# A state space scan on one core: its decay matrices made by small TensorE products in PSUM

## The chip, the core and the metric

The kernel runs on one core of a Trainium2 chip. The metric is the time of one execution in device microseconds. Before the change three runs took 1881.87 to 1888.46 us, with a median of 1887.11 us.

## What is computed

One layer of a hybrid block over 1024 tokens of width 1024, with 256 context tokens in front of the state space branch: a norm, three parallel branches (a bidirectional Mamba-2 scan, a Fourier mixing and a spatial gating), their gated merge, and a gated MLP. The change touches the scan alone. Its core, for one direction:

```python
def ssd_scan(x, dt, a, bm, cm, init_state, with_y):
    xf = (x.astype(jnp.float32) * dt[..., None]).reshape(b, nc, Q, G, R, P)
    la = jnp.transpose((dt * a).reshape(b, nc, Q, G, R), (0, 3, 4, 1, 2))
    cum = jnp.cumsum(la, axis=-1)
    ...
    tri_q = jnp.tril(jnp.ones((Q, Q), dtype=bool))
    lmat = jnp.exp(jnp.where(tri_q, cum[..., :, None] - cum[..., None, :], -jnp.inf))
    cb = jnp.einsum('bcqgn,bcsgn->bcgqs', cf, bf)
    y_diag = jnp.einsum('bcgqs,bgrcqs,bcsgrp->bcqgrp', cb, lmat, xf)
    y_off = jnp.einsum('bcqgn,bcgrpn,bgrcq->bcqgrp', cf, prev, jnp.exp(cum))
    y = (y_diag + y_off).reshape(b, L, H, P)
    return y.astype(x.dtype), final

def ssd_bidir(xs, bm, cm, dt, a_log, init_f, init_b, with_y):
    a = -jnp.exp(a_log.astype(jnp.float32))
    flip = lambda t: jnp.flip(t, axis=1)
    y_f, s_f = ssd_scan(xs, dt[:, :, 0], a[0], bm, cm, init_f, with_y)
    y_b, s_b = ssd_scan(flip(xs), flip(dt[:, :, 1]), a[1], flip(bm), flip(cm), init_b, with_y)
```

There are 16 heads in two groups of eight, and eight chunks of 128 tokens. lmat is the decay matrix: one 128 x 128 matrix for each head, chunk and direction.

## The kernel before

Activations lie with channels on the 128 partitions and tokens along the row. A big product is one output tile of 128 channels by 1024 tokens: eight slices of the inner dimension, each as three fp32r products (high by high, high by low, low by high) of two halves of 512 columns, 48 products in all (`mm3`, lines 147 to 157). It accumulates in a tile of two PSUM banks, `ps_big`, from a pool of two such tiles. psx, psf, psz, psu and psv are such accumulators: convolution inputs of the scan (psx), the Fourier branch (psf), the scan's gate (psz) and the two halves of the spatial gating (psu, psv). The weights come through `win`, which loads a tile, rounds it on ScalarE and takes the low part on GpSimd.

The scan runs in `ssd_group`, once per group of heads. Per chunk c it forms pcb (B by C of the chunk, L550), cbm (pcb under both triangular masks, L552), the contribution of the running state (`y_off`: po on TensorE, times the exponentiated rows ro, L514 to L519), and for each half group hg of four heads the weights E: rows of cumulated decays, broadcast over all partitions, come from memory by `rload` (rf and rs, L495); each head gets ScalarE L561, VectorE L562 (the smaller of both directions' exponents), ScalarE L564 and VectorE L565 (G: the masked cb times the step sizes of both directions). One Exp (L567), one multiplication on GpSimd (L568), and four heads of products into py (L573). Then y is added (L576), and the states of both directions go one chunk further (`state_step`, pS on TensorE L527, GpSimd L524 and L529, VectorE L531); the backward direction works on chunk 7 - c in the same turn. The row vectors ro have two buffers, the loads of x for the backward direction (Xb) one.

The order on each engine is not that of the text: a scheduler rearranges the instructions of the whole program by a model of their times, within what buffers and data allow, and each engine then works through its list in order. Buffers of a pool go to the tiles in the order in which the text allocates them. In the text `ssd_group(0)` comes first, then `group_in(1)` (psx9, psf0, psx11, psf1, psx4, psf2, psx5, psf3, psx6, psx7), then `ssd_group(1)`, then psz0 to psz3, psu0 to psu3 and psv0 on. Ahead of `ssd_group(0)` stand the last context tile (psc7) and `ctx_state`, which makes four start states through one tile and stores each (Std).

## Time and profile before

| | |
|---|---|
| median of three runs | 1887.11 us |
| the profiled execution, its own time | 1883.76 us |
| its span | 1882.0 us |
| TensorE busy | 1747.4 us, 93% |
| VectorE busy | 1383.9 us, 74% |
| ScalarE busy | 859.9 us, 46% |
| GpSimd busy | 856.0 us, 45% |
| the scan, from its first ro row to the last py | 231 to 554 us |

Engines are named PE (TensorE), DVE (VectorE), ACT (ScalarE), POOL (GpSimd) and SPq (the queue that issues all DMAs) in rows. A busy time sums the durations of an engine's instructions; neighbours on TensorE overlap, so a product's duration is longer than its distance to the next. "Idle before" is the time an engine stood before an instruction, with what ended it. A row of the timeline gives the start, the duration, the engine, the line, what was written from what, and how many.

### The profile page before, as it was taken

To read this page: it belongs to the slowest core of one execution; us is meant where nothing else is said; L and a number is where in the kernel's file an instruction comes from. 1 tells how busy PE (TensorE), PEld (TensorE's weight loads), DVE (VectorE), ACT (ScalarE), POOL (GpSimd) and SP (SyncE) were. 2 spreads that over 40 slices of the span, in tenths; PEclk is the share of its full clock that TensorE was granted. 3 is DMA by queue.
4 is the path that set the end of the run, shared out by engine and by line. 5 is a ranking of instruction groups with operands and counts; after the bars stand their busy time and mean duration, and the time that the engine had idled before them with its cause. 6 is when DMAs were issued, how large, how long until landed. Compare 5 with 4: busy or idle time off the path is not lost. (4 is left out here: it accounts for less than half of the span.)

```text
span 1882.0 us, 23647 instructions
## 1 busy us (share of the span) xinstructions
PE 1747.4 (93%) x8148; PEld 1409.2 (75%) x8148; DVE 1383.9 (74%) x1983; ACT 859.9 (46%) x1480; POOL 856.0 (45%) x579
## 2 busy tenths in 40 slices
...
GB/s 336 101 59 61 118 191 159 154 159 116 148 183 160 107 85 184 235 224 184 118 146 201 129 230 140 40 90 96 95 126 104 96 96 174 199 187 106 174 111 90
DMA packets 148064, 268.75 MB, mean 143 GB/s; under 512 B 15836, under 2 KB 56668, under 8 KB 146536
## 3 DMA queue, kind: packets, MB, share of 16 engines
...
## 5 line engine op out<-in xcount | busy, mean ns | idle before, releaser
L293 DVE SCALAR_TENSOR_TENSOR acc<-psx,convw,acc 128x1023 f32<-128x1023 f32 (+1 forms) x48 | 61.3, 1277 | 22.5 <-ACT acc L289 22.1
L562 DVE SCALAR_TENSOR_TENSOR rf<-rs,ncuml,rf 128x128 f32<-128x128 f32 x128 | 52.2, 454 | 32.4 <-ACT rf L561 29.2
L1272 POOL TENSOR_TENSOR pwo<-rwo,pwo 128x512 fp32r<-128x512 f32 x32 | 46.8, 1467 | 48.5 <-ACT pwo L1271 43.4
L857 POOL TENSOR_TENSOR w1up<-A11up,w1up 128x512 fp32r<-128x512 f32 x20 | 26.8, 1342 | 89.8 <-ACT w1up L856 80.6
L568 POOL TENSOR_TENSOR rf<-rf,G 128x512 f32<-128x512 f32 x32 | 46.1, 1442 | 43.1 <-DVE G L565 33.0
L857 POOL TENSOR_TENSOR w7up<-S3up,w7up 128x512 fp32r<-128x512 f32 x20 | 28.8, 1438 | 77.5 <-ACT w7up L856 45.0
L565 DVE SCALAR_TENSOR_TENSOR G<-cbm,dtl,G 128x128 f32<-128x128 f32 x128 | 57.0, 504 | 5.1 <-ACT G L564 5.1
L1561 DVE SCALAR_TENSOR_TENSOR xf<-Yd,g,xf 128x512 f32<-128x512 f32 x64 | 47.1, 743 | 13.0 <-PE Yd L867 12.7
L561 ACT ACTIVATE rf<-rf,ncuml 128x128 f32<-128x128 f32 x128 | 41.1, 389 | 29.5 <-DMA rf<-Rd 29.3
L166 ACT ACTIVATE gh<-gr 128x1024 fp32r<-128x1024 f32 (+1 forms) x36 | 37.1, 1034 | 38.0 <-DMA gr<-Gd 37.1
L157 PE MATMUL pso<-mh,pwo 128*128 128x512 f32 x128 | 50.2, 392 | 0.0
L153 PE MATMUL pso<-mh,pwo 128*128 128x512 f32 x128 | 49.8, 390 | 0.0
L155 PE MATMUL pso<-ml,pwo 128*128 128x512 f32 x128 | 49.8, 389 | 0.0
L517 DVE TENSOR_TENSOR scr<-po,ro 128x512 f32<-128x512 f32 x32 | 21.8, 683 | 35.2 <-ACT ro L504 35.0
L527 PE MATMUL pS<-scr,Bt 128*128 128x512 f32 x56 | 32.9, 671 | 15.4 <-DVE scr L517 12.0
L504 ACT ACTIVATE ro<-ro 128x512 f32<-128x512 f32 x32 | 20.1, 627 | 57.4 <-DMA ro<-Rd 57.1
L564 ACT ACTIVATE G<-cbm,dtl 128x128 f32<-128x128 f32 x128 | 39.6, 388 | 7.4 <-DVE cbm L552 7.4
L167 DVE TENSOR_TENSOR gl<-gr,gh 128x1024 fp32r<-128x1024 f32 (+1 forms) x26 | 39.7, 1527 | 4.2 <-ACT gh L166 3.6
L1477 DVE TENSOR_TENSOR gt<-gt,aa 128x512 f32<-128x512 f32 x44 | 42.5, 967 | 0.1
L1474 ACT ACTIVATE ft<-aa 128x512 f32<-128x512 f32 x44 | 27.8, 631 | 30.0 <-DVE aa L1456 29.0
L529 POOL TENSOR_TENSOR st<-st,etl 128x512 f32<-128x512 f32 x24 | 26.5, 1106 | 31.6 <-DVE st L531 31.6
L857 POOL TENSOR_TENSOR w4up<-A22up,w4up 128x512 fp32r<-128x512 f32 x20 | 30.9, 1544 | 21.4 <-ACT w4up L856 21.4
...
## 6 DMA issues: line engine op xcount, KB each, us to landing
gr<-Gd SPq DMA_DIRECT2D x70, 256.0 KB, 3.7
...
wm<-in_wmod_dram SPq DMA_DIRECT2D x16, 512.0 KB, 9.6
...
rf<-Rd SPq DMA_DIRECT2D x32, 256.0 KB, 4.3
rs<-Rd SPq DMA_DIRECT2D x32, 256.0 KB, 3.8
ctanh<-in_wmod_dram SPq DMA_DIRECT2D x32, 256.0 KB, 4.3
crow<-in_wmod_dram SPq DMA_DIRECT2D x32, 256.0 KB, 4.4
```

Source lines behind the costliest of these rows:

```text
L153: PE.matmul(o, wh[:, k, :], xh[:, sl], start=st, stop=False)
L155: PE.matmul(o, wh[:, k, :], xl[:, sl], start=False, stop=False)
L157: last_op["mm"] = PE.matmul(o, wl[:, k, :], xh[:, sl], start=False, stop=sp)
L293: V.scalar_tensor_tensor(acc[:, lo:hi], ps[:, lo + o:hi + o], cw[:, t, j:j + 1], acc[:, lo:hi], op0=ALU.mult, op1=ALU.add)
L561: S.activation(E[:, h, :], E[:, h, :], AF.Identity, bias=ncum[:, c, f:f + 1])
L562: V.scalar_tensor_tensor(E[:, h, :], rs[:, h, :], ncum[:, c, 16 + f:17 + f], E[:, h, :], op0=ALU.add, op1=ALU.min)
L565: V.scalar_tensor_tensor(Gm[:, h, :], cbm[:, 1, :], dtl[:, c, 16 + f:17 + f], Gm[:, h, :], op0=ALU.mult, op1=ALU.add)
L568: G.tensor_tensor(E, E, Gm, op=ALU.mult)
L857: (V if p in on_v else G).tensor_tensor(t[:, 1, :], ap, f32(t)[:, 0, :], op=ALU.subtract)
L1272: G.tensor_tensor(t[:, 1, :], raw, f32(t)[:, 0, :], op=ALU.subtract)
L1477: V.tensor_tensor(gt[:, 2 * q + h, :], gt[:, 2 * q + h, :], aa[:, HS[h]], op=ALU.mult)
L1561: V.scalar_tensor_tensor(xv, src, g2[:, dd:dd + 1], xv, op0=ALU.mult, op1=ALU.add)
```

## The change

The exponents of all heads of a half group are made by TensorE. For each direction ScalarE copies a mask (0 where a pair of tokens counts, -1e30 where not, the tile neg) into one PSUM bank of E, and a product of 18 rows adds to it, without clearing, for every pair of tokens the cumulated decay of the one (rows of Rt, high and low part, broadcast by rows of ones in Lt) and the logarithm of the step size less the cumulated decay of the other (rows of Lt, high and low part, picked per head by rows of Rt). The logarithm is taken once before the scan (lds). So the step size is in the exponent, and per half group there remain two mask copies and two Exp on ScalarE, one sum of the directions and one multiplication by cb on VectorE. rf, rs, cbm, G as it was, and lines 561 to 568 go. E is now a `ps_big` tile, from the same pool of two as the big products' accumulators. Lt is loaded once per group by eight loads, two rows of Rt per chunk and direction by one load each.

```diff
@@ -489,11 +489,14 @@
             filler()
         return BT, Bt, CT
 
-    def rload(c, d_, g, hg, nm, tag):
-        r = s3.tile([P, 4, P], F32, tag=tag, name=f"{nm}{g}{c}{hg}")
-        o = d_ * 16 + g * 8 + hg * 4
-        SY.dma_start(r, Rd[c, o:o + 4, :].partition_broadcast(P))
-        return r
+    def quad(c, d_):
+        return 32 * (2 * (c % 2) + d_)
+
+    def exponents(E, c, d_, hg, Lt):
+        q = quad(c, d_)
+        o = E[:, 512 * d_:512 * d_ + 512]
+        PE.matmul(o, Lt[q:q + 18, c // 2, :], Rt[q:q + 18, 512 * hg:512 * hg + 512], start=False, stop=True,
+                  skip_group_check=True)
 
     def decay_rows(c, d_, g):
         r = s3.tile([P, 4, P], F32, tag="ro", name=f"ro{d_}{g}{c}")
@@ -544,33 +547,42 @@
         stf, stb = st0
         scr[0, g] = tpool.tile([P, L], F32, tag="zz", name=f"scr0{g}", bufs=1)
         scr[1, g] = s3.tile([P, L], F32, tag="scr", name=f"scr1{g}", bufs=1)
+        Lt = s3.tile([P, 4, P], F32R, tag="Lt", name=f"Lt{g}", bufs=1)
+        S.activation(Lt, bc(ones.unsqueeze(1), [P, 4, P]), AF.Copy)
+        for c in range(2):
+            for d_ in range(2):
+                for l_ in range(2):
+                    q, o = quad(c, d_) + 8 * l_, d_ * 16 + g * 8
+                    SY.dma_start(f32(Lt)[q:q + 8], Rr[1][l_, c::2, o:o + 8, :].rearrange("c h q -> h c q"))
         for c in range(NCH):
             X = xload(g, c, "f")
+            for d_ in range(2):
+                q, o = quad(c, d_), d_ * 16 + g * 8
+                SY.dma_start(f32(Rt)[q + 16:q + 18], Rr[0][:, c, o:o + 8, :].rearrange("l h q -> l (h q)"))
             pcb = ps_small(f"pcb{g}{c}", "c")
             PE.matmul(pcb[:, 0:P], BT[:, c * P:(c + 1) * P], CT[:, c * P:(c + 1) * P], start=True, stop=True)
-            cbm = s3.tile([P, 2, P], F32, tag="cbm", name=f"cbm{g}{c}", bufs=1)
-            V.tensor_tensor(cbm, bc(pcb[:, 0:P].unsqueeze(1), [P, 2, P]), msk, op=ALU.mult)
+            cb = s3.tile([P, P], F32, tag="cb", name=f"cb{g}{c}")
+            S.activation(cb, pcb[:, 0:P], AF.Copy)
             y_off(g, c, 0, stf, CT, G)
             py = ps_small(f"py{g}{c}", "y")
             for hg in range(2):
-                E = rload(c, 0, g, hg, "rf", "rf")
-                rs = rload(c, 1, g, hg, "rs", "rs")
-                Gm = s3.tile([P, 4, P], F32, tag="G", name=f"G{g}{c}{hg}")
-                for h in range(4):
-                    f = g * 8 + hg * 4 + h
-                    S.activation(E[:, h, :], E[:, h, :], AF.Identity, bias=ncum[:, c, f:f + 1])
-                    V.scalar_tensor_tensor(E[:, h, :], rs[:, h, :], ncum[:, c, 16 + f:17 + f], E[:, h, :],
-                                           op0=ALU.add, op1=ALU.min)
-                    S.activation(Gm[:, h, :], cbm[:, 0, :], AF.Copy, scale=dtl[:, c, f:f + 1])
-                    V.scalar_tensor_tensor(Gm[:, h, :], cbm[:, 1, :], dtl[:, c, 16 + f:17 + f], Gm[:, h, :],
-                                           op0=ALU.mult, op1=ALU.add)
-                S.activation(E, E, AF.Exp)
-                G.tensor_tensor(E, E, Gm, op=ALU.mult)
+                E = ps_big(f"E{g}{c}{hg}")
+                for d_ in range(2):
+                    S.activation(E[:, 512 * d_:512 * d_ + 512].rearrange("p (h q) -> p h q", h=4),
+                                 bc(neg[:, d_].unsqueeze(1), [P, 4, P]), AF.Copy)
+                    exponents(E, c, d_, hg, Lt)
+                ef = s3.tile([P, 512], F32, tag="ef", name=f"ef{g}{c}{hg}")
+                eb = E[:, 512:1024]
+                S.activation(ef, E[:, 0:512], AF.Exp)
+                S.activation(eb, eb, AF.Exp)
+                V.tensor_tensor(eb, ef, eb, op=ALU.add)
+                w_ = s3.tile([P, 4, P], F32, tag="G", name=f"G{g}{c}{hg}")
+                V.tensor_tensor(w_, eb.rearrange("p (h q) -> p h q", h=4), bc(cb.unsqueeze(1), [P, 4, P]), op=ALU.mult)
                 for h in range(4):
                     hd = (4 * hg + h) * 64
                     j = h % 2
                     i = 2 * hg + h // 2
-                    PE.matmul(py[64 * j:64 * j + 64, i * P:(i + 1) * P], X[:, hd:hd + 64], E[:, h, :],
+                    PE.matmul(py[64 * j:64 * j + 64, i * P:(i + 1) * P], X[:, hd:hd + 64], w_[:, h, :],
                               start=True, stop=True)
             yv = y_view(g, c)
             V.tensor_tensor(yv, py.rearrange("p (i q) -> p i q", i=4), yv, op=ALU.add)
@@ -597,13 +609,27 @@
     xbc_post(10, psb10, CT)
     n2w, nfw, ssdd, ssdn, fcw, fcb = late_consts()
     Rd = dram.tile([NCH, 32, P], F32, name="Rd")
+    Rr = [dram.tile([2, NCH, 32, P], F32, name=f"Rr{i}") for i in range(2)]
     psr = ps_small("psr")
-    for i in range(2):
-        PE.transpose(out=psr[:, i * P:(i + 1) * P], in_=cums[:, 4 * i:4 * i + 4, :].rearrange("p c h -> p (c h)"),
+    lds = ddp.tile([P, NCH, 32], F32, name="lds", tag="w" + "l")
+    V.tensor_scalar(lds, dtl, 1e-37, None, op0=ALU.max)
+    S.activation(lds, lds, AF.Ln)
+    V.tensor_tensor(lds, lds, cums, op=ALU.subtract)
+    for i in range(4):
+        PE.transpose(out=psr[:, i * P:(i + 1) * P],
+                     in_=(cums, lds)[i // 2][:, 4 * (i % 2):4 * (i % 2) + 4, :].rearrange("p c h -> p (c h)"),
                      identity=ident)
+    pr4 = psr.rearrange("p (i q) -> p i q", i=4)
     Rs_ = ddp.tile([P, 2, P], F32, tag="ul", name="Rs_")
-    S.activation(Rs_, psr[:, 0:2 * P].rearrange("p (i q) -> p i q", i=2), AF.Copy)
+    S.activation(Rs_, pr4[:, 0:2], AF.Copy)
     SY.dma_start(Rd.rearrange("(i c) h q -> (c h) i q", i=2), Rs_)
+    for j in range(2):
+        rh = ddp.tile([P, 2, P], F32R, tag=("rl", "t2l")[j], name=f"rh{j}")
+        rl = ddp.tile([P, 2, P], F32R, tag=("ql", "lal")[j], name=f"rl{j}")
+        S.activation(rh, pr4[:, 2 * j:2 * j + 2], AF.Copy)
+        V.tensor_tensor(rl, pr4[:, 2 * j:2 * j + 2], f32(rh), op=ALU.subtract)
+        for q, t in enumerate((rh, rl)):
+            SY.dma_start(Rr[j][q].rearrange("(i c) h q -> (c h) i q", i=2), f32(t))
     yacc[0] = mpool.tile([P, 4, L], F32, tag="m", name="yacc0")
     for i, ts in enumerate(((9,), (4, 5), (6,), (7,))):
         x_tile(0, i, True)
@@ -616,6 +642,12 @@
     ctxp.release()
     ddp.release()
     s3 = pool("s3", bufs=2, side="right")
+    neg = s3.tile([P, 2, P], F32, name="neg", bufs=1)
+    V.tensor_scalar(neg, msk, -1.0, 1e30, op0=ALU.add, op1=ALU.mult)
+    Rt = s3.tile([P, L], F32R, name="Rt", bufs=1)
+    ind = s3.tile([P, L], F32, tag="scr", name="ind", bufs=1)
+    SY.dma_start(ind, a["ind"])
+    S.activation(Rt, ind, AF.Copy)
     ssd_group(0, *gi)
     with tc.issue_after(last_op["state"].ins):
         V.tensor_scalar(fcw[:, 0:NFF, :], fcw[:, 0:NFF, :], 0.5, None, op0=ALU.mult)
```

The last part of the diff, which is left out here, makes the table ind on the host: ones at the rows of Rt that pick a head.

TensorE in group 0, around the first chunk, as it was (psf1 and psx4 are big products):

```order
L153 MATMUL psx4_2708<-hh0_289,wx4h_2703 128x512 x2
L155 MATMUL psx4_2708<-hl0_290,wx4h_2703 128x512 x2
L157 MATMUL psx4_2708<-hh0_289,wx4l_2704 128x512 x2
L153 MATMUL psx4_2708<-hh1_326,wx4h_2703 128x512 x2
L573 MATMUL py00_1686<-rf000_1687,Xf00_1669 64x128 x4
L155 MATMUL psx4_2708<-hl1_327,wx4h_2703 128x512
L527 MATMUL pS107_1762<-scr10_1668,Bt0_591 128x512
L155 MATMUL psx4_2708<-hl1_327,wx4h_2703 128x512
L527 MATMUL pS000_1743<-scr00_1667,Bt0_591 128x512
L573 MATMUL py00_1686<-rf001_1714,Xf00_1669 64x128 x4
L157 MATMUL psx4_2708<-hh1_326,wx4l_2704 128x512 x2
```

And now, around chunks 3 and 4:

```order
L498 MATMUL E030_1953<-Rt_1685,Lt0_1695 128x512
L530 MATMUL pS104_2004<-scr10_1694,Bt0_591 128x512
L498 MATMUL E030_1953<-Rt_1685,Lt0_1695 128x512
L530 MATMUL pS003_1985<-scr00_1693,Bt0_591 128x512
L585 MATMUL py02_1876<-G021_1901,Xf02_1857 64x128 x4
L517 MATMUL po103_2070<-CT0_592,st104_2006 128x128 x4
L563 MATMUL pcb04_2013<-CT0_592,BT0_590 128x128
L498 MATMUL E031_1968<-Rt_1685,Lt0_1695 128x512
L517 MATMUL po004_2021<-CT0_592,st003_1987 128x128 x4
L498 MATMUL E031_1968<-Rt_1685,Lt0_1695 128x512
L585 MATMUL py03_1952<-G030_1962,Xf03_1933 64x128 x4
```

Before, the scan's products stand singly between those of psf1 and psx4. Now they follow each other: from pcb00, the first, to py07, the last, no row of a big product lies between them, and psx9 is the first big product behind psc7.

TensorE at the end of psx7's transposes, as it was (py07 is the last chunk of group 0, psz1 a big product):

```order
L157 MATMUL psz1_4012<-hh2_363,wz1l_4008 128x512 x2
L153 MATMUL psz1_4012<-hh3_400,wz1h_4007 128x512
L445 MATMUL pstx71_3127<-cst_95,acc7_3110 128x128 x4
L153 MATMUL psz1_4012<-hh3_400,wz1h_4007 128x512
L155 MATMUL psz1_4012<-hl3_401,wz1h_4007 128x512 x2
L157 MATMUL psz1_4012<-hh3_400,wz1l_4008 128x512 x2
L573 MATMUL py07_2372<-rf070_2373,Xf07_2355 64x128 x4
L573 MATMUL py07_2372<-rf071_2400,Xf07_2355 64x128 x4
L550 MATMUL pcb10_3142<-CT1_2444,BT1_2442 128x128
L153 MATMUL psz1_4012<-hh4_437,wz1h_4007 128x512 x2
```

And now, right behind the last product of psx7:

```order
L498 MATMUL E100_3030<-Rt_1685,Lt1_3000 128x512
L445 MATMUL pstx60_2902<-cst_95,acc6_2891 128x128 x4
L498 MATMUL E100_3030<-Rt_1685,Lt1_3000 128x512
L445 MATMUL pstx61_2908<-cst_95,acc6_2891 128x128 x4
L498 MATMUL E101_3045<-Rt_1685,Lt1_3000 128x512
L498 MATMUL E110_3106<-Rt_1685,Lt1_3000 128x512
L498 MATMUL E101_3045<-Rt_1685,Lt1_3000 128x512
L445 MATMUL pstx70_2981<-cst_95,acc7_2970 128x128 x4
L498 MATMUL E110_3106<-Rt_1685,Lt1_3000 128x512
L445 MATMUL pstx71_2987<-cst_95,acc7_2970 128x128 x4
L498 MATMUL E111_3121<-Rt_1685,Lt1_3000 128x512 x2
L585 MATMUL py10_3029<-G100_3039,Xf10_3010 64x128 x4
```

Group 0's scan used to reach into psz1, where group 1's began. Now group 1's scan starts behind psx7, and psz0 is the next big product, between the two halves of py17.

The queue of DMA issues around chunk 4, as it was (ro: rows for y_off, by direction, group and chunk; rf, rs: rows for E; Xf, Xb: x of a chunk):

```order
L503 DMA ro104_2042<-Rd_865 64x4x128 x2
L503 DMA ro004_2067<-Rd_865 64x4x128 x2
L495 DMA rf030_1981<-Rd_865 128x512
L495 DMA rf031_2008<-Rd_865 128x512
L536 DMA Xf04_2061<-Xd0_580 128x512
L536 DMA Xb02_2249<-Xd0_580 128x512
L495 DMA rs040_2081<-Rd_865 128x512
L471 DMA Xd1_581<-xt4_2767 128x8x128
L495 DMA rs041_2108<-Rd_865 128x512
L503 DMA ro103_2140<-Rd_865 64x4x128 x2
L495 DMA rf040_2079<-Rd_865 128x512
```

And now:

```order
L539 DMA Xb03_2077<-Xd0_580 128x512
L561 DMA Rt_1685<-Rr0_866 2x1024
L506 DMA ro004_2017<-Rd_865 64x4x128 x2
L506 DMA ro103_2066<-Rd_865 64x4x128 x2
L539 DMA Xb02_2153<-Xd0_580 128x512
L539 DMA Xf04_2009<-Xd0_580 128x512
L561 DMA Rt_1685<-Rr0_866 2x1024
L506 DMA ro005_2093<-Rd_865 64x4x128
L561 DMA Rt_1685<-Rr0_866 2x1024
L506 DMA ro005_2093<-Rd_865 64x4x128
L506 DMA ro102_2142<-Rd_865 64x4x128 x2
```

The loads of rf and rs are gone, Rt has come in, and the four loads of ro004 and ro103 stand together.

VectorE at the same place now (E, G: the two steps of a half group; st: states):

```order
L580 TENSOR_TENSOR G030_1962<-E030_1953,cb03_1939 128x512
L520 TENSOR_TENSOR scr10_1694<-po103_2070,ro103_2066 128x512
L520 TENSOR_TENSOR scr00_1693<-po004_2021,ro004_2017 128x512
L578 TENSOR_TENSOR E031_1968<-ef031_1973,E031_1968 128x512
L534 TENSOR_TENSOR st103_2082<-st103_2082,pS103_2080 128x512
L580 TENSOR_TENSOR G031_1977<-E031_1968,cb03_1939 128x512
L534 TENSOR_TENSOR st004_2063<-st004_2063,pS004_2061 128x512
L588 TENSOR_TENSOR yacc0_892<-py03_1952,yacc0_892 128x4x128
```

The products with ro of both directions (scr10, scr00) stand ahead of the sum E031, where before the steps of L562 and L565 stood.

## Rows read from the trace of the kernel before

**Rows 1.** Windows: busy us (count) of PE, PEld, DVE, ACT, POOL; clock; DMA.

```profile
100.00:190.00 90.00, 85.47 (x501) 74.85 (x500) 60.32 (x100) 37.90 (x59) 20.27 (x9) 0.96 0.21 66
...
230.00:558.00 328.00, 293.83 (x1479) 221.23 (x1478) 232.34 (x418) 172.68 (x382) 178.23 (x128) 0.96 0.53 154
700.00:900.00 200.00, 200.00 (x884) 165.56 (x883) 123.49 (x226) 88.19 (x150) 100.61 (x72) 1.00 0.61 200
```

**Rows 2.** Timeline of TensorE: first big product beside the scan, first psF product.

```profile
190.12 0.63 PE L153 MATMUL psx<-hh,wx9h 128*128 128x512 f32 x2
...
558.01 1.24 PE L707 MATMUL psF<-tabc,fT 128*128 128x128 f32 x9
```

**Rows 3.** Groups by line, 190 to 558 us, TensorE: busy, mean ns.

```profile
L527 PE MATMUL pS<-scr,Bt 128*128 128x512 f32 x56 | 32.9, 671 | 15.4 <-DVE scr L517 12.0 <-POOL scr L524 3.4
L514 PE MATMUL po<-CT,st 128*128 128x128 f32 x224 | 31.9, 290 | 6.4 <-DVE st L531 4.5 <-DVE cbm L552 1.7
L573 PE MATMUL py<-rf,Xf 128*64 128x128 f32 x256 | 20.4, 284 | 5.5 <-POOL rf L568 5.5
```

**Rows 4.** Groups by line, 230 to 560 us, VectorE, GpSimd and ScalarE.

```profile
L565 DVE SCALAR_TENSOR_TENSOR G<-cbm,dtl,G 128x128 f32<-128x128 f32 x128 | 57.0, 504 | 5.1 <-ACT G L564 5.1
L562 DVE SCALAR_TENSOR_TENSOR rf<-rs,ncuml,rf 128x128 f32<-128x128 f32 x128 | 52.2, 454 | 32.4 <-ACT rf L561 29.2 <-DMA rs<-Rd 2.9
L293 DVE SCALAR_TENSOR_TENSOR acc<-psx,convw,acc 128x1023 f32<-128x1023 f32 (+1 forms) x20 | 25.5, 1277 | 4.7 <-ACT acc L289 4.6
L517 DVE TENSOR_TENSOR scr<-po,ro 128x512 f32<-128x512 f32 x32 | 21.8, 683 | 35.2 <-ACT ro L504 35.0 <-issue 0.2
...
L568 POOL TENSOR_TENSOR rf<-rf,G 128x512 f32<-128x512 f32 x32 | 46.1, 1442 | 43.1 <-DVE G L565 33.0 <-PE psx L157 6.2 <-DVE rf L562 3.1
L529 POOL TENSOR_TENSOR st<-st,etl 128x512 f32<-128x512 f32 x24 | 26.5, 1106 | 31.6 <-DVE st L531 31.6
...
L561 ACT ACTIVATE rf<-rf,ncuml 128x128 f32<-128x128 f32 x128 | 41.1, 389 | 29.5 <-DMA rf<-Rd 29.3
L504 ACT ACTIVATE ro<-ro 128x512 f32<-128x512 f32 x32 | 20.1, 627 | 57.4 <-DMA ro<-Rd 57.1 <-ACT rf L561 0.3
```

**Rows 5.** Timeline: last context convolution; stores of start states and loads waiting for them.

```profile
195.59 1.36 DVE L298 SCALAR_TENSOR_TENSOR cacc<-ctmp,cacc 128x256 f32<-128x256 f32 x2 [0.23 <-ACT ctmp L297]
...
211.28 0.33 SPq L411 DMA_DIRECT2D Std<-ctxm  x1
213.29 0.32 SPq L543 DMA_DIRECT2D st00i<-Std  x1
...
218.31 0.32 SPq L411 DMA_DIRECT2D Std<-ctxm  x1
222.24 0.32 SPq L543 DMA_DIRECT2D st10i<-Std  x1
```

**Rows 6.** Timeline around the ro rows of one turn: VectorE, queue, ScalarE.

```profile
247.63 1.27 DVE L517 TENSOR_TENSOR scr<-po,ro 128x512 f32<-128x512 f32 x2
248.33 2.84 SPq L503 DMA_DIRECT2D ro<-Rd  x4
...
252.43 0.63 ACT L504 ACTIVATE ro<-ro 128x512 f32<-128x512 f32 x1 [1.09 <-DMA ro<-Rd]
254.49 0.63 ACT L504 ACTIVATE ro<-ro 128x512 f32<-128x512 f32 x1 [1.43 <-DMA ro<-Rd]
```

**Rows 7.** DMA issues, 240 to 550 us: KB each, median us to landing.

```profile
Xf<-Xd SPq DMA_DIRECT2D x14, 256.0 KB, 5.6
...
Xd<-xt SPq DMA_DIRECT2D x4, 512.0 KB, 3.5
```

**Rows 8.** Windows of 2 us around an idle stretch; columns as in rows 1.

```profile
402.00:404.00 2.00, 0.00 (x0) 0.00 (x0) 2.00 (x4) 2.00 (x6) 1.24 (x2) 1.00 0.64 199
...
406.00:408.00 2.00, 2.00 (x4) 0.93 (x3) 2.00 (x2) 0.61 (x1) 2.00 (x2) 0.50 0.70 217
```

4 lines of the change are left out of this document (added).

## The prediction

> **What bounds the kernel now.** I read the windows first. From 700 to 900 us TensorE is busy all the time, 884 products in 200 us, 0.226 us each; in the stretch of the scan, 230 to 558 us, it is busy 294 of 328 us, and VectorE only 232, ScalarE 173, GpSimd 178 [rows 1]. TensorE bounds this stretch too, with 34 us of holes. The timeline shows why: the big product psx9 starts at 190.12, the moment the last context product ends, and from there to 558.01, where psF starts, twenty big products (psx9, psf0, psx11 ... psv1) stand between the scan's small ones [rows 2]. The stretch takes 367.9 us. The holes are waits for the scan's chain: 12.0 us of TensorE's wait before pS go to VectorE's scr [rows 3], which itself stood 35.0 us behind the row vectors ro, and ScalarE 57.1 us behind their loads [rows 4].
>
> **What the change takes away.** On VectorE L562 and L565 go, 52.2 and 57.0 us; on ScalarE L561 (41.1 us) and its twin L564; on GpSimd L568 (46.1 us) [rows 4]; on the queue 64 broadcast loads rf and rs. None of these engines is the bound here, so this is worth at most part of the 34 us of holes.
>
> **What it adds.** Per half group of four heads: two mask writes to PSUM and two Exp on ScalarE, two adds or multiplies on VectorE, two products of 18 rows on TensorE. Before the scan come one Ln, its neighbours and four small stores; ScalarE is busy 37.9 of 90 us there, GpSimd 20.3 [rows 1], and the big products cover them: nothing. That cover would cost a few us if the decay chain were late; in the built order it feeds nothing before the scan.
>
> **What it moves is the main term.** E is allocated from the pool of two that holds the accumulators of the big products. In the built order of the changed kernel every product of E, po, py and pS of group 0 now stands in one piece on TensorE, behind psc7 and before psx9; those of group 1 stand between psx7 and psz0. TensorE works its queue in order, so the scan has nothing left to hide behind: the twenty products and the scan are added instead of overlapped. I sum the same stretch, from the end of psc7 to the end of psv1.
>
> Products: 20 x 48 x 0.226 = 217 us, and 6 for the transposes and small sums between them: 223.
>
> Start-up of group 0. The last context convolution ends at 195.59 + 1.36 = 197; transposes, copies, one weighting and one product add 2.5. Then four context states follow each other through one tile: two VectorE steps (2 x 0.68 as in L517 [rows 4]) and a store that must land. A load that waits for that store starts 2.0 us after it in one case and 3.9 in the other [rows 5]; I take 3.0, so three full rounds of 4.4 and a last 1.4, to 214. VectorE writes the mask tile neg only behind them; the queue issues the last state, eight loads of Lt and two of Rt (0.32 each [rows 5], then some 3.5 to land as for Xd [rows 7]): first product of E at about 221. Masks, ro, two Exp per tile, four VectorE steps: the first chunk's second E is consumed at 230. In all 40 us (32 if states land in 2.0 and the queue does not hold, 46 at 3.9 with the row loads late). Today psx9, psf0 and psx11 lie over all of it.
>
> Turn-around before group 1: after psx7 four convolution steps of 1.28 [rows 4], activation and gate, transposes and two copies, some 10 us; the store Xd 3.5, the load Xf 5.6 at most [rows 7], of which I take 4.5; the first two chunks, whose E are ready, 5.5. In all 23.5 (20 to 27).
>
> One chunk alone, T. TensorE: two pS at 32.9/28, two po at 31.9/32, two halves of py at 20.4/32 [rows 3], pcb 0.25, four E at 0.226: 6.8 us. VectorE: ten steps of 0.68, 6.8. ScalarE: ten of 0.63 and one of 0.39, 6.7. GpSimd: five of 1.1, 5.5 [rows 4]. Four nearly full engines in order, and a loop over them: ro has two buffers; a buffer is free when VectorE has multiplied it; four loads follow on the queue; the later row is exponentiated; VectorE multiplies both. The trace has this once undisturbed: issue of four at 248.33, the second Exp at 254.49 for 0.63, so 6.8 us; two multiplies take 1.27 [rows 6]: 8.1. In the new order one Rt load of 0.35 stands between them: 8.4. I take T = 8.4, since it is the longest loop of which the trace shows every part. Below, 6.8 if landings hide; above, 10.4 if the rows land like Xf, 2.3 us later.
>
> Of eight chunks seven count in group 0 and six in group 1 (the others lie in the two terms above), and 1.7 us overlap at the ends. Sum: 223 + 40 + 23.5 - 1.7 + 13 x 8.4 = 394 us, against 367.9: 26 us more. The profiled execution took 1883.8 us (span 1882.0), so 1910; its time is 3.3 under the median of the three runs, which gives 1913. I predict 1911. The rest of the kernel is untouched.
>
> A smaller point is the form of the products. The 64 products of E use 18 rows at a quarter of the array, the others all rows. No row of before shows that change of shape; the nearest are the 128x64 halves of py, whose 0.64 us for eight [rows 3] leave no visible gap. So I charge nothing, and as an upper bound one product's 0.226 us for each of eight changes in a chunk, which puts TensorE at 8.6, just over the loop, and the time 3 us later. The Trainium skill (TensorEngine Tiling, Tiling Modes) says that changing the tiling mode drains the engine; by it the sum would move to that upper bound, and no run here shows it yet.
>
> **The rivals.** *The scan runs free.* Without big products in the queues, chains shorten until only the engines' own 6.8 us count. For it: GpSimd and VectorE lose their longest neighbours and the queue 64 loads. Against it: the loop over ro does not contain any of these. 13 x 6.8 gives 373 us, 1889.
>
> *Faster after all.* Equal time needs T = (367.9 - 284.8)/13 = 6.4 us. If products of TensorE overlap more than their busy times show (6.0 us in a chunk) and the start-up is 32 and the turn-around 20, the sum is 352: 1868. It decides when T falls under 6.4. Against it: TensorE and VectorE are both above 6.4 by rows, with no wait at all.
>
> *TensorE at half clock.* Idle from 402 to 404, TensorE is at 0.50 of its clock from 406 to 408, with four products in 2 us [rows 8]; that is 1.2 instead of 2.4 GHz. The start-up leaves it idle longer, and in the scan it works in short pieces. At the low clock its 6.8 us become near 12 (products of 512 columns double), it is the bound, and with T = 10.4 to 11.6 the time is 1936 to 1952. The loads of rows landing late end at the same times. Against it: in 230 to 558, with a tenth of the time idle, the mean clock is still 0.96 [rows 1]. The Trainium skill (TensorE: Matmul & The Clock Gate, What's actually happening) has the slow clock as the default that activity releases; the row of 406 to 408 agrees with it, with 0.50.
>
> **How the numbers follow.** The forecast (T from 7.1 to 9.6, 1893 to 1926): 0.66. The scan runs free (within 0.5% of the 1883.8, the least that a measurement of this kernel can tell from no change): 0.13. Faster: 0.05. Half clock or late rows: 0.16. So faster 0.05, same 0.13, slower 0.82. The range, with the bounds of T, start-up and turn-around: 1890 to 1944; it leaves out the faster case, the lower part of the free one and the end of the slow one.
>
> **What would show it.** Right: TensorE has no psx or psf product between about 190 and 288 us; the first E near 221; psx9 near 288, psx7's end near 401, psz0 near 474, psv1's end near 584; chunks of py 8 to 9 us apart; ScalarE waits before ro for a DMA; windows of products alone are full. The removed lines are gone and their gain is not in the time. Wrong: products of py under 7 us apart (the scan runs free), a granted clock well under 0.9 in the scan's stretches (half clock), or psx9 well before 270 us.

## The result and the profile after

The changed kernel takes 1948.1 us (median of four runs, 1940.7 to 1949.4) against 1887.8 for the kernel before on the same chip: 1.0315 times as long, 95% interval 1.0278 to 1.0352. Slower, as forecast, but by 60 us instead of 24, and 4 us above the range. The profiled execution has a span of 1947.6 us. Medians here and below are of fast executions alone; one slow execution of e15_serial_min (2027.3 us, mean granted clock 0.857) is left out.

The timeline of TensorE shows the order that was forecast. Columns: start, us, engine, line, operation, out<-in, shapes, count, [idle before, what ended it].

```profile
191.68 0.28 PE L157 MATMUL psc<-hch,wc7l 128*128 128x256 f32 x1
...
222.74 1.19 PE L498 MATMUL E<-Rt,Lt 18*128 18x512 f32 x2 [4.02 <-DMA Rt<-Rr]
...
303.20 1.22 PE L153 MATMUL psx<-hh,wx9h 128*128 128x512 f32 x2
...
309.08 0.66 PE L585 MATMUL py<-G,Xf 128*64 128x128 f32 x8
...
420.14 0.61 PE L157 MATMUL psx<-hh,wx7l 128*128 128x512 f32 x2
...
428.43 0.79 PE L498 MATMUL E<-Rt,Lt 18*128 18x512 f32 x1 [4.71 <-ACT E L571]
...
442.23 1.98 PE L585 MATMUL py<-G,Xf 128*64 128x128 f32 x16 [1.82 <-DMA Xf<-Xd]
...
449.79 1.09 PE L585 MATMUL py<-G,Xf 128*64 128x128 f32 x16
...
509.54 1.22 PE L153 MATMUL psz<-hh,wz0h 128*128 128x512 f32 x2
...
626.42 0.61 PE L157 MATMUL psv<-hh,wv1l 128*128 128x512 f32 x2
```

The order as told ahead of the prediction is wrong in one detail: the second half of py07 (309.08) stands inside psx9, as that of py17 stands inside psz0.

From the end of psc7 (192.0) to that of psv1 (627.0) it is 435.0 us: 67 more than the 367.9 of before [rows 2], of which the rest of the program gives 1.5 back; 41 more than the forecast's 394. Where these 41 lie:

| piece | forecast, us | measured, us |
|---|---|---|
| psc7's end to the first chunk's w (VectorE L580, 231.7) | 40 | 39.7 |
| rest of group 0's scan, to psx9 | 58 | 71.5 |
| products psx9 to psx7 | 111.5 | 117.5 |
| turn-around with group 1's first two chunks, to VectorE's second sum of py (L588, 452.0) | 23.5 | 31.2 |
| group 1's other six chunks, to psz0 | 49.5 | 57.6 |
| products psz0 to psv1 | 111.5 | 117.5 |

The two pieces of the scan are 22 us longer, the turn-around 8, the products 12. VectorE's sum of py (L588) comes once per chunk. From one to the next it takes 8.0 to 15.3 us in group 0 and 7.7 to 13.0 in group 1; the means of the seven intervals are 10.96 and 10.51, where 8.4 was forecast. The last interval of a group reaches into psx9 or psz0, so these means lie a little above what a chunk costs in the sum. "Per chunk" below is always this, and two numbers are the two groups.

Windows of the changed kernel, as in [rows 1] (length, then busy time and count of PE, PEld, VectorE, ScalarE, GpSimd; granted clock; DMA share, GB/s):

```profile
222.00:230.00 8.00, 5.59 (x8) 2.07 (x8) 3.38 (x6) 4.86 (x9) 3.27 (x3) 0.50 0.52 167
232.00:242.00 10.00, 8.88 (x57) 5.89 (x57) 7.46 (x12) 7.10 (x15) 7.49 (x8) 1.00 0.50 145
250.00:258.00 8.00, 7.78 (x23) 3.48 (x24) 5.01 (x8) 4.32 (x9) 4.09 (x5) 0.59 0.35 99
260.00:270.00 10.00, 9.79 (x60) 5.92 (x60) 6.65 (x11) 6.86 (x14) 5.88 (x6) 1.00 0.37 107
272.00:280.00 8.00, 5.59 (x31) 3.56 (x31) 5.08 (x9) 3.44 (x8) 4.27 (x5) 0.92 0.39 122
280.00:300.00 20.00, 17.97 (x62) 10.17 (x62) 9.09 (x17) 10.59 (x20) 5.03 (x4) 0.50 0.27 80
320.00:420.00 100.00, 99.32 (x457) 81.95 (x457) 30.77 (x26) 32.28 (x35) 19.11 (x8) 1.00 0.24 79
430.00:440.00 10.00, 5.36 (x13) 2.84 (x13) 3.80 (x5) 7.37 (x13) 1.79 (x1) 0.50 0.20 57
```

The clock column is the news. The scan starts at 0.50 (1.2 GHz) behind the idle start-up, comes to 1.00 (2.4 GHz), and falls back to 0.50 after stretches with holes (272 to 280: 5.59 of 8 us busy). In 280 to 300 TensorE is busy 17.97 of 20 us and does 62 products; at 1.00 it did 60 in 10 us. The last row of the next fence shows it on one product: pS takes 2.08 us at 0.50 (279.75) and 1.10 at full clock (269.84). The Trainium skill (TensorE: Matmul & The Clock Gate, What's actually happening) calls the slow clock the default that activity releases; these rows agree. The products alone, 320 to 420, run full.

One chunk at full clock, TensorE without a hole, and a pS at the low clock:

```profile
265.90 0.66 PE L585 MATMUL py<-G,Xf 128*64 128x128 f32 x8
266.49 0.49 PE L563 MATMUL pcb<-CT,BT 128*128 128x128 f32 x2
266.91 0.50 PE L498 MATMUL E<-Rt,Lt 18*128 18x512 f32 x1
267.56 1.16 PE L517 MATMUL po<-CT,st 128*128 128x128 f32 x8
268.64 0.49 PE L498 MATMUL E<-Rt,Lt 18*128 18x512 f32 x1
269.20 0.66 PE L585 MATMUL py<-G,Xf 128*64 128x128 f32 x8
269.84 1.10 PE L530 MATMUL pS<-scr,Bt 128*128 128x512 f32 x2
270.87 0.49 PE L498 MATMUL E<-Rt,Lt 18*128 18x512 f32 x1
271.29 1.13 PE L530 MATMUL pS<-scr,Bt 128*128 128x512 f32 x2
272.35 0.49 PE L498 MATMUL E<-Rt,Lt 18*128 18x512 f32 x1
272.76 1.16 PE L517 MATMUL po<-CT,st 128*128 128x128 f32 x8
273.85 0.66 PE L585 MATMUL py<-G,Xf 128*64 128x128 f32 x8
...
279.75 2.08 PE L530 MATMUL pS<-scr,Bt 128*128 128x512 f32 x2
```

From py to py it is 7.95 us, not the 6.8 of the sum. Each E holds TensorE for 0.41 to 0.65 us, to the start of the next product (266.91 to 267.56, 270.87 to 271.29), not 0.226: 2.0 us for four instead of 0.9. Groups by line, 230 to 303 us (busy, mean ns | idle before, what ended it):

```profile
L498 PE MATMUL E<-Rt,Lt 18*128 18x512 f32 x28 | 16.2, 606 | 3.0 <-ACT E L571 3.0
...
L571 ACT ACTIVATE E<-neg 128x512 f32<-128x512 f32 x27 | 15.8, 594 | 6.1 <-PE E L498 5.9
...
L507 ACT ACTIVATE ro<-ro 128x512 f32<-128x512 f32 x16 | 10.0, 626 | 9.2 <-DMA ro<-Rd 9.2
...
L576 ACT ACTIVATE ef<-E 128x512 f32<-128x512 f32 x14 | 8.3, 592 | 13.8 <-PE E L498 13.8
```

The removed lines are gone as expected. But ScalarE's longest wait is not for ro, as in [rows 4]; it is for TensorE's E (13.8 and 5.9 us), and TensorE in turn waits for ScalarE's masks.

### The profile page after: what moved, and what is told of

Read it like the earlier page. It is cut to its first block, busy times and chain, and to the rows that moved or that the text cites. A ratio compares the mean times of both kernels' runs of the same rounds, so it can differ in the third digit from the quotient of the medians.

```text
span 1947.6 us, 23376 instructions
## 1 busy us (share of the span) xinstructions
PE 1799.8 (92%) x8214; PEld 1433.5 (74%) x8214; DVE 1304.2 (67%) x1780; ACT 843.9 (43%) x1344; POOL 805.0 (41%) x547
## 5 line engine op out<-in xcount | busy, mean ns | idle before, releaser
L498 PE MATMUL E<-Rt,Lt 18*128 18x512 f32 x64 | 36.6, 602 | 23.1 <-ACT E L571 19.0
L1593 DVE SCALAR_TENSOR_TENSOR xf<-Yd,g,xf 128x512 f32<-128x512 f32 x64 | 47.2, 743 | 12.8 <-PE Yd L899 12.6
L571 ACT ACTIVATE E<-neg 128x512 f32<-128x512 f32 x64 | 37.5, 593 | 24.0 <-PE E L498 17.3
L498 PEld LDWEIGHTS E<-Rt,Lt 18*128 18x128 f32 x64 | 13.5, 218 | 46.4 <-ACT E L571 30.5
L517 PEld LDWEIGHTS po<-CT,st 128*128 128x128 f32 x224 | 30.9, 212 | 13.9 <-issue 5.8
L530 PE MATMUL pS<-scr,Bt 128*128 128x512 f32 x56 | 38.2, 774 | 2.1 <-DVE scr L520 1.8
L517 PE MATMUL po<-CT,st 128*128 128x128 f32 x224 | 35.2, 307 | 5.1 <-ACT cb L565 4.9
L1507 DVE SCALAR_TENSOR_TENSOR aa<-ft,aa 128x512 f32<-128x512 f32 x44 | 36.9, 839 | 1.9 <-ACT ft L1506 1.7
L897 PE MATMUL Yup<-bhh,w7up 128*128 128x512 f32 x80 | 32.1, 401 | 6.5 <-DVE Uup L1088 6.5
```

The costliest lines, as they stand in the source:

```text
L498: PE.matmul(o, Lt[q:q + 18, c // 2, :], Rt[q:q + 18, 512 * hg:512 * hg + 512], start=False, stop=True, skip_group_check=True)
L517: PE.matmul(po[:, i * P:(i + 1) * P], st[:, i * P:(i + 1) * P], CT[:, c * P:(c + 1) * P], start=True, stop=True)
L530: PE.matmul(p_, Bt[:, c, :], xw.rearrange("p h q -> p (h q)"), start=True, stop=True)
L1593: V.scalar_tensor_tensor(xv, src, g2[:, dd:dd + 1], xv, op0=ALU.mult, op1=ALU.add)
```

## The experiments

All kernels but b1_serial are the changed kernel with the edit shown or named; b1_serial is the kernel before with an edit. The kernel before took 1887 to 1889 us beside every run. A scan is called bare where no big products stand between its own; runs that set scan and big products side by side again are called mixed. Per-chunk times and rows come from one profiled execution of each run, which lay within 5 us of the median except in e4_pemask (1934.9 us) and e10_fill (1979.1).

| run | median, us | ratio to before, 95% | us per chunk, groups 0 and 1 |
|---|---|---|---|
| changed kernel | 1948.1 | 1.028 to 1.035 | 10.96, 10.51 |
| b1_serial | 1969.3 | 1.040 to 1.047 | 14.82, 15.33 |
| e6_ro4 | 1946.4 | 1.028 to 1.034 | 11.02, 9.89 |
| e4_pemask | 1944.4 | 1.025 to 1.036 | 9.50, 9.63 |
| e4c_mask4 | 1978.1 | 1.045 to 1.053 | 11.85, 12.08 |
| e8b_k128_pe | 1931.1 | 1.019 to 1.027 | 8.56, 9.16 |
| e8a_k128 | 1952.5 | 1.031 to 1.037 | 9.67, 10.09 |
| e10_fill | 1970.7 | 1.043 to 1.049 | 11.51, 12.14 |
| e7b_onemask | 1924.3 | 1.017 to 1.023 | 8.12, 10.27 |
| e13_fill | 1936.2 | 1.023 to 1.028 | 9.85, 9.98 |
| e15_serial_min | 1944.6 | 1.027 to 1.032 | 10.55, 10.80 |
| e5_pemask_banks | 1948.4 | 1.028 to 1.036 | mixed |
| e9_bank_t | 1943.8 | 1.027 to 1.035 | mixed |
| e9b_bank_t_pe | 1941.6 | 1.025 to 1.033 | mixed |
| e12_two | 1939.5 | 1.026 to 1.031 | mixed |
| e14b_min_t | 1924.0 | 1.017 to 1.022 | mixed |
| e14c_min_c | 1919.5 | 1.014 to 1.019 | mixed |
| e14_min | 1935.3 | 1.021 to 1.029 | mixed |

### Is it the order? The old arithmetic in the new order

```diff
-            pcb = ps_small(f"pcb{g}{c}", "c")
+            pcb = ps_big(f"pcb{g}{c}")
```

> The kernel before, old arithmetic, with one word changed: pcb, one small product per chunk, is allocated in the pool of the big products. In its built order the scan of a group then stands in one piece behind psc7 and behind psx7, as in the changed kernel. Theory 1 (lost overlap): the old arithmetic alone is bound by VectorE, 11.3 us per chunk by its rows, and half clock on TensorE costs nothing there; 1930 to 1965 us. Rival (where the scan stands matters little, the loss is the new arithmetic's): 1880 to 1900 us.

1969.3 us, 82 above before and 4 above the first theory's range, by an edit of one word. In the windows VectorE is the bound of the bare scan:

```profile
250.00:270.00 20.00, 14.31 (x76) 8.37 (x75) 18.82 (x34) 11.43 (x32) 13.34 (x12) 0.84 0.65 165
```

So the order by itself costs the old arithmetic more than the whole change does, and in nearly that order the new arithmetic is 21 us faster. The orders are not quite the same: here the products of py of each group's last three chunks stand between big products again, from 304 and 523 us on. A chunk takes 14.8 and 15.3 us, not 11.3; in 250 to 300 us L565 takes 694 ns, against 504 before [rows 4], and why is open.

### The step of the prediction: the loop over ro

```diff
-        r = s3.tile([P, 4, P], F32, tag="ro", name=f"ro{d_}{g}{c}")
+        r = s3.tile([P, 4, P], F32, tag="ro", ...) if d_ == 0 else \
+            tpool.tile([P, 2, 4, P], F32, tag="acc", ...)[:, 0]
```

> The changed kernel with four buffers for the row vectors ro instead of two (those of the backward direction in a tile of the convolutions' pool). Theory of the prediction (the loop over ro's two buffers sets the 8.4 us per chunk): the loop is gone, TensorE's own 7 to 8 us are left, 10 to 18 us less than the changed kernel's 1948, 1930 to 1938 us. Rival (TensorE bounds the scan at either clock; the loop over ro is just below it): within 6 us of 1948, with ScalarE's wait for ro gone and its waits for TensorE larger.

1946.4 us, as the rival said: the two buffers don't set the pace. But ScalarE's wait for ro did not go, though both theories said so; from the waits of this run, 230 to 300 us (in total, how often, longest):

```profile
PEld E L498 <- ACT E L572: 13.7, 12, 2.6
ACT ro L508 <- DMA ro<-Rd: 11.1, 8, 2.4
```

What holds these loads was not tried. The waits for the masks are of the same size: TensorE's weight loads (PEld) stood 13.7 us for them, its products 8.9.

### The masks as products, and what one product of E costs

```diff
-                    S.activation(E[...], bc(neg[:, d_]...), AF.Copy)
+                    PE.matmul(E[...], idr, bc(neg[:, d_]...), start=True, stop=False)
```

e4_pemask has this once per half tile, e4c_mask4 four times. e8b_k128_pe is e4_pemask with

```diff
-        PE.matmul(o, Lt[q:q + 18, c // 2, :], Rt[q:q + 18, ...], ...)
+        PE.matmul(o, Lt[c % 2][:, 4 * d_ + c // 2, :], Rt2[c % 2][:, ...], ...)
```

> The changed kernel, with the mask of each half tile of E written by one more TensorE product (identity times mask tile, 128 rows, 512 columns, start) instead of a copy on ScalarE. Per chunk TensorE gets 4 products of 0.226 us at full clock more, ScalarE 4 copies of 0.63 us less. The changed kernel took 10.3 us per chunk, and its granted clock fell to 0.50 in 250 to 258 and 278 to 306 us. Theory 1 (half clock): at full clock a chunk takes 8.0 to 8.4 us, at half clock 13, and the clock falls because TensorE is left waiting; fewer holes, so more of the scan at full clock, 8.4 to 9.5 us per chunk: 1923 to 1938 us, with less than a third of the scan at 0.50. Theory 2 (the chain mask, product, Exp between ScalarE and TensorE sets the pace, whatever the clock): 4 copies and 4 handovers go out of the chain, 7.5 to 8.5 us per chunk, 1912 to 1925 us, with the clock still at 0.50 in as much of the scan.

> As the run with mask products, but each mask product is given four times (each starts anew, so the result is the same): 12 products of 0.226 us more per chunk for TensorE, 2.7 us at full clock, 5.4 at half. Theory 1 (holes on TensorE bring the clock down): the holes are filled, the granted clock stays at 0.9 or more through the scan, a chunk takes TensorE's 6.8 + 0.9 + 2.7 = 10.4 us, and the time is the changed kernel's 1948 us within 10 us, although 150 products more are in it than with one mask product. Theory 2 (the clock does not depend on it): 2.7 to 5.4 us per chunk on top of the run with one mask product, 1955 to 1995 us, with the clock at 0.50 in as much of the scan as there.

> As the run with mask products in the changed kernel's order (1944 us), but E's products read 128 rows, with zeros outside their 18 (same result; Lt in two tiles of the pool of the convolutions, Rt in two tiles in turn, four small loads more at a group's start). In that run a product of E stood 0.43 us, four mask products in a row 0.226 each and 0.2 after the last. Theory 1 (each change between 18 and 128 rows costs TensorE 0.2 us): eight changes per chunk less, 1.6 us, TensorE bounds the scan, 13 chunks: 15 to 21 us less, 1923 to 1932 us, and E's products 0.23 us apart. Rival (0.43 is the wait for the mask product in the same bank, not the rows): no gain, 1940 to 1952 us, spacing still 0.43.

Timelines of TensorE, first e4c_mask4:

```profile
261.72 1.20 PE L571 MATMUL E<-neg,idr 128*128 128x512 f32 x4
262.85 0.50 PE L498 MATMUL E<-Rt,Lt 18*128 18x512 f32 x1
263.28 1.19 PE L571 MATMUL E<-neg,idr 128*128 128x512 f32 x4
```

then e8b_k128_pe:

```profile
254.47 0.40 PE L498 MATMUL E<-Rt,Lt 128*128 128x512 f32 x1
254.71 0.40 PE L575 MATMUL E<-neg,idr 128*128 128x512 f32 x1
254.94 0.40 PE L498 MATMUL E<-Rt,Lt 128*128 128x512 f32 x1
255.18 1.05 PE L516 MATMUL po<-CT,st 128*128 128x128 f32 x8
```

Four products of 128 rows and the change to 18 rows take 1.13 us (261.72 to 262.85); four times 0.226 is 0.90. The product of 18 rows then holds TensorE for 0.43. With 128 rows it is 0.24. So each change of rows costs 0.2 us. The Trainium skill (TensorEngine Tiling (Array Packing), Tiling Modes) says that changing the tiling mode drains the engine; these rows agree and give the price. The rival, a wait for the mask in the same bank, falls: there too the mask stands just ahead of E. Over the program the edit took 13 us (1944.4 to 1931.1, in the first theory's range; the intervals of the two ratios overlap a little), 0.9 and 0.5 us per chunk.

e4_pemask itself saved only 4 us, less than its four executions differ (1934.9 to 1955.2), and lies outside both theories' numbers: ScalarE's four copies went, but TensorE got four products and their changes of rows, and a chunk takes 9.5 us with TensorE busy 19 of 20 us. Its clock stays at 1.00 in 12 of 14 chunks. e4c_mask4 is not what its first theory said: the clock stays up, yet 12 products more add 2.4 us per chunk, nearly their full 2.7, and the time lies in the second theory's range. TensorE bounds this scan at full clock.

e8a_k128 is the edit to 128 rows in the changed kernel itself.

> The changed kernel itself (masks by ScalarE), with E's products over 128 rows, zeros outside their 18. In the run with mask products the same edit took 13 us away, and a product of E after a mask product stood 0.23 us instead of 0.43. Theory 1 (the change of rows is TensorE's own time, and TensorE bounds the scan): 8 changes per chunk, 13 us again, 1930 to 1938 us, less up to 4 us back in the turn-around, since Lt now waits for the last convolutions. Rival (with ScalarE's masks TensorE waits around every E anyway, so the change of rows is hidden in those waits): 1943 to 1950 us.

1952.5 us, no gain, and inconclusive as a test of the theory: the chunks are 1.3 and 0.4 us shorter, 12 us in all, but the first sum of py comes 6.7 us later in group 0 and 7.1 later behind psx7; that Lt's zeros and loads lengthen the start of each group would fit, and was not shown.

### Clock or waits?

A handover is a place where one engine waits for what another has written into a tile. e10_fill keeps ScalarE's masks and puts a product ahead of each, to keep TensorE busy:

```diff
+                    PE.matmul(E[...], idr, bc(neg[:, d_]...), start=True, stop=True)
                     S.activation(E[...], bc(f32(neg)[:, d_]...), AF.Copy)
```

> The changed kernel, with one product of 128 rows and 512 columns put into each half of E's bank ahead of ScalarE's mask, which then overwrites it. All of the changed kernel's handovers stay and one from TensorE to ScalarE is added; TensorE gets 64 products more. Theory 1 (TensorE's holes bring its clock down, and the low clock is a large part of the loss): the granted clock stays above 0.9 in most of the scan (the changed kernel's was 0.50 for 44 of the 82 us from 222 to 304), and the time is no higher than the changed kernel's 1948 us plus 8, although 64 products of 0.43 us and a handover each are added. Rival (the handovers set the pace, the clock only follows): each E waits for one product more, 13 chunks by 4 by 0.5 us: 1970 to 1980 us, whatever the clock.

```profile
240.70:321.20 80.50, 70.22 (x335) 41.76 (x335) 45.68 (x71) 40.52 (x76) 32.95 (x30) 0.87 0.31 92
457.90:542.90 85.00, 74.89 (x334) 44.33 (x335) 45.64 (x69) 35.21 (x67) 33.58 (x31) 0.82 0.27 79
```

These are the two groups, from the first sum of py to the last. The same stretches of the changed kernel:

```profile
233.17:309.87 76.70, 67.34 (x307) 39.91 (x307) 44.35 (x72) 39.54 (x77) 33.98 (x31) 0.78 0.34 96
444.30:517.90 73.60, 63.49 (x314) 38.64 (x315) 45.12 (x68) 34.52 (x67) 33.17 (x32) 0.87 0.32 91
```

The time is the rival's, 1970.7. But the clock rose in group 0 alone (0.78 to 0.87) and fell in group 1 (0.87 to 0.82), so the fill did not keep it up, and the run does not tell clock from waits. e7b_onemask then halves the handovers and sets the products of E in pairs:

```diff
-                for d_ in range(2):
-                    S.activation(E[half d_], bc(neg[:, d_]...), AF.Copy)
-                    exponents(E, c, d_, hg, Lt)
+                S.activation(E, bc(neg...), AF.Copy)
+                for d_ in range(2):
+                    exponents(E, c, d_, hg, Lt)
```

> The changed kernel, with the masks of both halves of a tile of E in one copy of 1024 columns on ScalarE and the two products of E behind it, next to each other. TensorE waits for ScalarE half as often, and changes rows four times in a chunk instead of eight. Theory 1 (waits for masks and changes of rows): half of the 23 us that TensorE stood idle before E go, and four changes of some 0.15 us per chunk, 8 us: 1928 to 1940 us. Rival (the loop runs over E's two tiles, whose parts now come later): 1944 to 1956 us.

1924.3 us: 24 less, the most of the runs with a bare scan, and 4 below the first theory's range. The edit does two things, and no run parts them. TensorE's timeline:

```profile
253.19 0.50 PE L498 MATMUL E<-Rt,Lt 18*128 18x512 f32 x2
253.61 1.12 PE L530 MATMUL pS<-scr,Bt 128*128 128x512 f32 x2
```

Both products of E take 0.42 us together, as long as one did. They use different quarters of the array's rows; the Trainium skill (TensorEngine Tiling (Array Packing), Tiling Modes) says that different tiles can execute in parallel, and this row agrees. Windows of the same kernel in its two groups:

```profile
252.00:262.00 10.00, 9.35 (x59) 5.44 (x58) 8.99 (x16) 6.89 (x11) 7.42 (x7) 1.00 0.48 143
440.00:450.00 10.00, 7.33 (x36) 5.08 (x35) 5.57 (x10) 5.00 (x8) 6.27 (x6) 0.66 0.40 114
```

The same program takes 8.12 us per chunk in group 0, at 1.00, and 10.27 in group 1, where three chunks ran at 0.65 to 0.74 and took 10.7, 13.6 and 13.1. e13_fill asks which comes first. It adds to e7b_onemask one product per half chunk that nobody reads:

```diff
+                kp = ps_small(f"kp{g}{c}{hg}", "t")
+                PE.matmul(kp, w_[:, 0, :], w_.rearrange("p h q -> p (h q)"), start=True, stop=True)
```

> As the run with one mask copy for both halves (1924 us), with one product more per half chunk that nobody reads: 128 rows, 512 columns, float32, on the weights w that the py behind it reads, into the idle tile t. By pS (two passes of 0.43 us) it takes TensorE 0.86 us at full clock, 1.7 us per chunk, and it stands where TensorE has work anyway. In the run without it chunks at a granted clock of 1.00 took 8.1 us on average, those under 0.75 took 10.7, 13.6 and 13.1. Theory 1 (the low clock makes those chunks long): TensorE is kept at work, the clock stays at 0.95 or more in both groups, a chunk takes 8.1 plus up to 1.0 us: 1912 to 1928 us. Rival (long waits make those chunks long, and the clock falls because of them): every chunk gets 1 to 1.7 us longer, 1937 to 1950 us.

1936.2 us, just under the rival's range, but the groups differ. Group 0, at 1.00 before and 0.98 now, pays for the work: 8.12 to 9.85, 1.73 us per chunk. Group 1, from the first sum of py to the last, in e7b_onemask and then in e13_fill:

```profile
421.60:493.50 71.90, 59.33 (x306) 37.59 (x307) 43.84 (x68) 33.30 (x55) 33.49 (x32) 0.83 0.32 93
439.20:509.10 69.90, 62.56 (x339) 36.40 (x340) 43.88 (x69) 33.27 (x55) 34.11 (x32) 0.99 0.33 96
```

It has the same work added, its clock rose from 0.83 to 0.99, and it is no longer than before: 10.27 and 9.98 us per chunk. The added products keep TensorE busy for 14.8 us of it. Its other busy time fell from 59.3 to some 48 us, its idle time from 12.6 to 7.3. So, as an estimate from one execution of each, the holes took up 5 us of the added work, and the higher clock gave back some 11, or 1.6 us per chunk. The low clock costs time of its own and is not only a mark of long waits.

e15_serial_min takes the masks' handover away otherwise: no mask in PSUM, VectorE caps the exponent.

```diff
+                    V.tensor_tensor(e_, E[half d_], bc(neg[:, d_]...), op=ALU.min)
+                    S.activation(e_, e_, AF.Exp)
```

> The changed kernel's order, with no mask in PSUM: the two products of E start their banks, and VectorE takes the minimum of each half and a cap (60 inside the triangle, -1e30 outside) into SBUF, where Exp, sum and product with cb follow. ScalarE loses four mask copies per chunk, VectorE gets four steps of 0.68 us, 9.5 us in all. Theory 1 (TensorE's and ScalarE's waits around the mask set the pace): a chunk falls to VectorE's 9.5 us or, where the steps overlap, less, and TensorE's idle time before E goes from 23 us to under 5: 1915 to 1932 us. Rival (VectorE's four more steps lie on the same chain): 1940 to 1960 us, with VectorE over 90% busy in the scan.

1944.6 us, the rival: VectorE is full, at 10.5 and 10.8 us per chunk.

```profile
270.00:290.00 20.00, 15.05 (x84) 10.00 (x82) 19.83 (x27) 6.96 (x14) 13.75 (x10) 0.83 0.33 98
```

### Giving the overlap back

Seven runs put scan and big products side by side again, by other PSUM tiles for E: in c and c2 (e5_pemask_banks, masks as products), alone in t with group 1's transposes moved to the big pool (e9_bank_t, and e9b_bank_t_pe with mask products), in t and c2 (e12_two); and the same with VectorE's cap in place of masks (e14c_min_c in c and c2, e14b_min_t in t, e14_min in t and c2).

```diff
-                E = ps_big(f"E{g}{c}{hg}")
+                E = [ps_small(f"E{g}{c}{hg}{d_}", ("c", "c2")[d_]) for d_ in range(2)]
```

> As the run with mask products, but E's two halves lie in the single-bank tiles c and c2 that the scan uses for pcb, po and pS, not in the pool of the big products. In its built order the scan's products stand between those of psx9 to psv1 again. Theory 1 (the loss is the lost overlap): the stretch comes back to the 368 us of before or less, 1865 to 1895 us, granted clock near 0.96 in the stretch. Rival (the new arithmetic costs it: products of 18 rows that TensorE has to change shape for, or longer chains): 1905 us or more, although the overlap is back.

> The changed kernel, with E in the single-bank tile t alone (forward and backward half one after the other, the sum in an SBUF tile), and the transposes of group 1 that had t moved to the pool of the big products. In the built order two or three scan products stand between every few products of psx11 to psv1, evenly, as before; the run with E in c and c2 had used up its big products early and was left with 49, 54 and 16 us of bare scan. Theory 1 (it is the order: a bare scan costs holes and half clock): TensorE's work is the 334 us that it is busy in the 368 us of before, plus 64 products of E at 0.43 us, the spacing at which they follow each other at full clock: 362 us, and with few holes 1880 to 1900 us, granted clock above 0.95 all through. Rival (the new arithmetic on TensorE itself is too dear, wherever it stands): 1915 us or more.

> As the run with E alone in the tile t, with the masks as TensorE products too (64 of 128 rows). Theory 1: 64 times 0.226 to 0.43 us more on TensorE, which bounds the stretch: 14 to 28 us above the run with ScalarE's masks, 1895 to 1925 us. Rival (handing the bank to ScalarE for the mask and back holds TensorE up more than the product): below the run with ScalarE's masks.

> As the run with E in the tile t, but with E's two halves in t and c2, and pcb, po and pS of both directions in c. In its built order the products of E stand in pairs, one to two chunks ahead of the py that uses them, between big products. Theory 1 (what that run lost are TensorE's 25 us of waits for ScalarE's masks, the changes of rows and the clock that fell in the holes): most of the waits and half of the changes go, 1895 to 1920 us. Rival (whatever order the products stand in, another of the mutual waits takes the place): 1930 to 1950 us.

> The cap on VectorE in place of the masks, with E in the single-bank tile t and the transposes of group 1 in the pool of the big products: scan and big products stand mixed, as in the run with E in t (1944 us). There TensorE waited 24.6 us for ScalarE's masks, and its clock was low for 62 us of work. Theory 1 (the masks' handover is what the mixed order lost): those waits go, the clock stays up, TensorE's 316 us of other work and 28 to 33 for E: 1885 to 1910 us. Rival (other waits take their place, VectorE's chain now among them): 1930 to 1950 us.

> The cap on VectorE in place of the masks, with E's halves in c and c2, the tiles of pcb, po and pS, and the transposes left where they are: the mixed order as in the run with mask products in c and c2 (1948 us), where TensorE had 31 us of mask products and bare scan of 49, 54 and 16 us at the groups' ends. Theory 1 (handover and mask products are what it lost): 31 us of products go and the bare ends stay in part, 1900 to 1920 us. Rival: 1935 to 1950 us.

> The cap on VectorE in place of the masks, E's halves in t and c2, pcb, po and pS of both directions in c, the transposes of group 1 in the pool of the big products. In its built order E stands one to two chunks ahead, group 0's scan ends before psz0 with no bare piece, group 1's last three chunks stand bare behind psv1. Theory 1 (what is left of the loss are bare ends at a low clock): 39 us of bare scan less than the run with E in c and c2 (1919 us), of which products that were already due take half: 1895 to 1908 us. Rival (TensorE's own time for E, 31 us in a stretch that TensorE bounds, is the rest of the loss): 1912 to 1930 us.

Not one came back to the time of before: 1948.4, 1943.8, 1941.6, 1939.5, 1924.0, 1919.5, 1935.3 us. The first theory fell in six of the seven; e14c_min_c lies at the upper end of its 1900 to 1920. The rival's numbers held in e5_pemask_banks, e9_bank_t and e12_two; e9b_bank_t_pe lies 2 us below e9_bank_t, which the noise allows, and e14b_min_t and e14_min met neither theory. Groups by line of e9_bank_t, 190 to 640 us:

```profile
L580 PE MATMUL E<-Rt,Lt 18*128 18x512 f32 x64 | 36.2, 566 | 24.6 <-ACT E L578 24.6
```

In the mixed order too TensorE is busy with E for 36 us, in a stretch where it is busy 412 of 460 us (190 to 650), and it waits 25 us for ScalarE's masks. With the cap those waits go, and e14c_min_c is the best of all, but its big products are used up before the scan is:

```profile
350.00:370.00 20.00, 20.00 (x108) 15.43 (x107) 11.74 (x14) 8.04 (x11) 5.79 (x4) 1.00 0.27 78
430.00:450.00 20.00, 14.60 (x54) 10.11 (x55) 18.10 (x20) 9.22 (x14) 7.70 (x6) 0.57 0.22 64
```

Up to 410 us TensorE is full at 1.00; then the scan stands bare, with VectorE at 18.10 of 20 us and a clock of 0.57; the end of group 1's scan, 550 to 590, runs at 0.59 to 0.67. e14_min was to remove that end in group 0 and was slower; why was not settled. No version beat the kernel before.

## Why the prediction was wrong

**Direction and order: right.** No big product stands between 192 and 303 us, and the start-up took 39.7 us of 40. That the order is the main term held for the old arithmetic (b1_serial, 82 us). For the new arithmetic it is not shown. Mixed, it took 1939.5 and 1943.8 us with ScalarE's masks (bare: 1948.1), 1941.6 and 1948.4 with mask products (1944.4), and 1919.5 to 1935.3 with the cap (1944.6). So giving the overlap back brought at most 25 of the 60 us. The mixed runs also put E into tiles that other products use, and what that costs was not parted from the rest.

**The term that was mis-sized most is T, 8.4 us per chunk.** By the terms of the sum it came out at 10.1: the two pieces of the scan, 71.5 and 57.6 us, with the 1.7 of overlap, over 13 chunks. That is 22 of the 41 us. (By the sums of py it is 10.7, which counts the ends inside psx9 and psz0 too.) Three things are in it. The loop over ro, on which 8.4 rested, is not the loop that sets it (e6_ro4); that the full-clock chunk of 7.95 us comes near it is chance. First, the price of E: "no visible gap" was read off halves that use all rows, and four E cost 2.0 us instead of 0.9. The bound that I put beside it, 0.226 us for each of eight changes of rows, was near the price: 0.2 in e4c_mask4, and 0.14 in the chunk above (7.95 less 6.8, over eight). The Trainium skill's rule (TensorEngine Tiling (Array Packing), Tiling Modes), which I weighed and didn't charge, is the one that held. Second, the handovers of the mask, product and Exp of E between ScalarE and TensorE, both in order, which I counted as busy time and not as waits: chunks at a clock of 0.94 or more took 9.7 us on average in the changed kernel (six, from 8.0 to 13.0), 8.4 in e7b_onemask with half the handovers and paired products. Third, the low clock: the eight chunks at 0.90 or less took 11.5 (from 7.7 to 15.3). As an estimate, it is worth at most 19 us here: TensorE is busy 38 us at 0.50 in these two pieces, and half of that is what the full clock could give back. No run parts the three for the changed kernel itself; the run that should (e10_fill) added a wait of its own and did not hold the clock up.

**The turn-around, 23.5 us, took 31.2.** It holds group 1's first two chunks. TensorE waited 4.71 us for a mask of E and 1.82 for Xf, so the first product of py started 21.5 us behind psx7's end, where 18 was forecast; from there to the second sum of py it is 9.8 us instead of 5.5, with the clock at 0.50 up to 446 us.

**The rival of half clock** was given 0.16 and a T of 10.4 to 11.6, 1936 to 1952 us. The time fell inside, T at 10.1 just below, and the sign set for it came: 0.78 and 0.87 over the two groups. Its mechanism was half right: the clock was low in a part of the chunks, not in all, and chunks at full clock lie above 8.4 too. What I held against it, a mean clock of 0.96 in [rows 1], was of a scan whose holes big products filled.

**The products' 223 us** took 235. The 960 products themselves took 224 instead of 217, from start to next start: psx9 and psz0 each begin at the low clock (1.22 us for the first two of psx9, 0.62 later). The small ones between them took 11 instead of 6.

**What the removed work is worth.** "None of these engines is the bound" was right for the old order, and in a bare scan wrong: there VectorE was (b1_serial), and the new arithmetic gains 21 us on it. Mixed again, the same arithmetic loses. That it moves work from engines with room to the one that has least fits the rows of e9_bank_t; no run shows it alone.
